# The fold's masked matrix made one pair earlier, PSUM evacuations more steps behind, and two expert downs moved to the end

## The chip, the cores and the metric

The kernel runs on one core of a Trainium2 chip. The metric is the device time of one execution in microseconds (us), the median of several runs. Profiles are of a single execution on that core.

## What is computed

A batch of 256 tokens with 1024 features goes through a first block (a mixer, attention to a memory, a layer of experts) and then two layers of a second block. The change concerns the experts of the first block alone:

```python
def hier_moe(h, w_rg, b_rg, w_re, b_re, w_gate, w_up, w_down):
    # every token picks 1 of 4 groups, in it 2 of 8 experts, with weights
    ...
    def expert_block(args):
        xb, e = args
        return (jax.nn.silu(xb @ w_gate[e]) * (xb @ w_up[e])) @ w_down[e]
    ...
    out = jnp.zeros((T, D), jnp.float32).at[t_sorted].add(contrib)   # weighted sum per token
```

There are 32 experts; w_gate and w_up are 1024x512 each, w_down 512x1024, all fp32. The second block's filters (sines of a small network, then a Fourier transform of 256 points as matrix products) depend on no token, and the kernel computes their spectra beside the experts.

## The kernel before

**Pairs.** Experts e and e+16 form a pair j (0 to 15). The 128 rows of a TensorE operand hold 64 slots of token features twice, rounded part and remainder, so that one pass over a weight gives both. `features` gathers tokens into the slots of four experts by a matmul with a 0/1 matrix `Dm` that `chosen` makes; its result is copied by ScalarE from PSUM to `XT`. `up` multiplies a pair's slots by gate (i = 0) and up (i = 1) weights, eight steps each; `gate` adds the two parts of the product and takes Silu into `G`, and `gated` multiplies `G` by the up product. `fold` is a matmul of `G` by a small matrix `F`: it transposes `G` and puts each slot to the expert it belongs to, since a crowded expert may use its partner's slots. `F` (128x128) is the table `fold` masked by `mine[:, j]`, two VectorE instructions. The fold's product is copied to `AT` as rounded part (ScalarE) and remainder (VectorE). `down` multiplies by the down weights in two halves of four steps; `result` copies each half to `Y`; `combine` multiplies `Y` by the weights and places of the tokens (`DT`, made by `weighted`: a VectorE mask, a transpose, a copy) into four PSUM sums that stay open over all pairs.

**Steps.** The work is emitted in 24 steps per pair j: 0 to 15 are `up(j)`, 16 to 23 `down(j-1)`. A step is: `go_on()`, which resumes delayed pieces that are due; `self.weights`, which asks for one weight half; four matmuls of 512 columns; then the pieces that `plan` holds for this step. A piece is a generator: `yield n` lets it go on n steps later. Within an engine the instructions run in the order in which they were emitted (`manual_schedule`).

**Weight halves.** A load brings 1 MB (128x2048 fp32) to one of nine places. Each half of it (128x1024) is split: ScalarE rounds it into `whi` (line 454, five buffers) and VectorE subtracts into `wlo` (line 455, four buffers). At step s the halves up to that of step s+4 have been asked for (`NH` = 5), so a piece started in the plan of step s stands on ScalarE and VectorE behind the half for step s+4, and one that `go_on` resumes at step s behind the half for step s+3. A place is loaded anew when both of its halves are split; the order of loads is the list `self.stream`, which follows `DOWN`.

**PSUM.** Four tiles `acc` hold the sums; two tiles `tp` serve features, transposes, folds and filters in turn; two tiles `misc` serve the products of `up` and `down` in turn.

**Slots of the plan.** `WHEN` gives the steps: features 6, 9, 12, 15 in even pairs and 14, 16, 18, 20 in odd ones; transposed weights from 1, 4, 7, 10 in pairs 1, 3, 7, 11; filter pieces at 8 and 14 of pairs 1 to 10; combines of pair j-2 at 3, 5, 7, 9; `fold(j-1)` at 0 and, for the last pair, at 16. A filter piece may issue loads on SyncE's queue (`decay`, lines 1280 and 1281) and stores on ScalarE's (lines 1315 and 1316, after a memset on VectorE, line 1314).

Lines to follow: 454 and 455 the split, 875 features' copy, 886 the masks for transposes, 899 to 909 gate and gated, 915 and 916 F, 921 the fold's matmuls, 927 and 929 its copies, 934 results, 940 combines, 960/961 and 977/978 the matmuls of up and down.

Of the kernel before, what the change touches and what calls it, by code (L numbers as in the profile page):

```python
# [22 lines left out]
F32 = mybir.dt.float32  # L23
# [4 lines left out]
OP = mybir.AluOpType  # L28
# [3 lines left out]
P = 128  # L32
# [3 lines left out]
SLOTS = 64  # L36
# [31 lines left out]
def _cols(v):  # L68
# [12 lines left out]
PAIRS = NE // 2  # L81
MEMBERS = [m * PAIRS + j for j in range(PAIRS) for m in range(2)]


WHEN = dict(features=((0, 6), (0, 9), (0, 12), (0, 15), (1, 14), (1, 16), (1, 18), (1, 20)), chosen=2,
            weighted=(1, 4, 7, 10), filters=(8, 14), combine=(3, 5, 7, 9))

DOWN = lambda j: (j - 1,) if j else ()


def _constants():
# [158 lines left out]
class Kernel:  # L250
# [246 lines left out]
    def block1(self, outer, moe):  # L497
# [3 lines left out]
        with ExitStack() as ctx:  # L501
# [218 lines left out]
            for j in range(PAIRS + 1):  # L720
                if j < PAIRS:
                    self.stream.extend(("w_egu", 8 * j + 4 * m + 2 * i + n)
                                       for i in range(2) for m in range(2) for n in range(2))
                for d in DOWN(j):
                    self.stream.extend(("w_ed", 4 * d + 2 * m + n) for n in range(2) for m in range(2))
# [86 lines left out]
    def moe(self, hh, hl, A, W):  # L812

        nc, tc = self.nc, self.tc
        mm = nc.tensor.matmul
        x = self.x
        with ExitStack() as ctx:
# [3 lines left out]
            a = ctx.enter_context(tc.tile_pool(name="moe", bufs=1, reuse_waits="tile"))  # L821
            rk = a.tile([P, 2, NE], F32, name="rk")
            mine = a.tile([P, PAIRS], F32, name="mine")
# [27 lines left out]
                    else:  # L851
                        start(work)

            XT, DT, Dms, G, AT, Y = {}, {}, {}, {}, {}, {}

            def chosen(q):

# [7 lines left out]
            def features(q, k):  # L865

                if k % 2 == 0:
                    XT[q].append(a.tile([P, 2, 4, 2, SLOTS], F32R, name="XT", bufs=6))
                ps = self.tp()
                for i, h in enumerate((hh, hl)):  # L870
                    for t in range(2):
                        mm(ps[:, i * S:(i + 1) * S], h[:, t, k * P:(k + 1) * P],
                           Dms[q][:, t].rearrange("p e j -> p (e j)"), start=t == 0, stop=t == 1)
                yield 1
                nc.scalar.activation(XT[q][k // 2][:, k % 2].rearrange("p e i j -> p i e j"),  # L875
                                     ps.rearrange("p (i e j) -> p i e j", i=2, j=SLOTS), AF.Copy)

            def weighted(o, t, h):


                if t == h == 0:
                    DT[o] = self.junk.tile([P, 4, S], F32, name="DT", tag="xn", bufs=2)
                Dw = a.tile([P, 2, 2, SLOTS], F32, name="Dw")
                for n in range(2):
                    j = 4 * o + 2 * h + n
                    nc.vector.tensor_scalar(Dw[:, n], self.c["slot"][:, None, :].to_broadcast([P, 2, SLOTS]),
                                            rp[:, t, j:j + 1], wp[:, t, j:j + 1], op0=OP.is_equal, op1=OP.mult)
                yield 2
                ps = self.tp()
                for n in range(2):  # L890
                    nc.tensor.transpose(ps[:, n * P:(n + 1) * P], Dw[:, n].rearrange("p i j -> p (i j)"), self.ident)
                yield 1
                nc.scalar.activation(DT[o][:, 2 * h:2 * h + 2, t * P:(t + 1) * P],
                                     ps[:, :2 * P].rearrange("p (n s) -> p n s", s=P), AF.Copy)

            def gate(j, p):
                yield 1
                z = a.tile([SLOTS, 512], F32, name="z")
                nc.scalar.activation(z, p[SLOTS:], AF.Copy)
                yield 1  # L900
                nc.vector.tensor_add(z, p[:SLOTS], z)
                yield 2
                G[j] = a.tile([P, 512], F32, name="g")
                for n in range(2):
                    nc.scalar.activation(G[j][n * SLOTS:(n + 1) * SLOTS], z, AF.Silu)

            def gated(j, p):
                yield 1
                nc.vector.tensor_mul(G[j], G[j], p)

            def fold(j):


                F = a.tile([P, 2, SLOTS], F32, name="F")
                nc.vector.tensor_scalar(F[:, 0], self.c["fold"], mine[:, j:j + 1], None, op0=OP.mult)
                nc.vector.tensor_sub(F[:, 1], self.c["fold"], F[:, 0])  # L916
                yield 2
                g = G.pop(j)
                pt = self.tp()
                for f in range(4):  # L920
                    mm(pt[:, f * P:(f + 1) * P], g[:, f * P:(f + 1) * P], F.rearrange("p m j -> p (m j)"),  # L921
                       start=True, stop=True)
                yield 1
                AT[j] = a.tile([P, 4, 2, 2, SLOTS], F32R, name="at", bufs=2)
                at = AT[j].rearrange("p f m i j -> p (f m) i j")
                pt = pt.rearrange("p (f j) -> p f j", j=SLOTS)
                nc.scalar.activation(at[:, :, 0], pt, AF.Copy)
                yield 1
                nc.vector.tensor_sub(at[:, :, 1], pt, at[:, :, 0].bitcast(F32))

            def result(j, n, p):
                yield 1
                Y[j, n] = a.tile([P, 512], F32, name="ye", bufs=2)
                nc.scalar.activation(Y[j, n], p, AF.Copy)

# [2 lines left out]
            def combine(j, t, n):  # L938

                mm(sums[t][n], DT[j // 4][:, j % 4, t * P:(t + 1) * P], Y[j, n], start=j == 0, stop=j == PAIRS - 1)  # L940
                yield 1

            def twice(work):
                n = 1
                while n:
                    n = next(work)
                    yield n
# [18 lines left out]
            def down(j, plan):  # L966
                at = AT.pop(j)
                for n in range(2):
                    p = self.misc()
                    for s in range(4):  # L970
                        m, h = divmod(s, 2)
                        go_on()
                        wh, wl = self.weights("w_ed", 8 * j + 4 * m + 2 * n + h)
                        for k in range(2):
                            l = at[:, 2 * h + k, m].rearrange("p i j -> p (i j)")
                            c = slice(k * 512, k * 512 + 512)
                            mm(p, l, wh[:, c], start=s == k == 0, stop=False)  # L977
                            mm(p, l, wl[:, c], start=False, stop=s == 3 and k == 1)  # L978
                        for work in plan[16 + 4 * n + s]:
                            start(work)  # L980
                    start(result(j, n, p))
# [14 lines left out]
            for j in range(PAIRS + 1):  # L996
                q, r = divmod(j, 2)
                plan = [[] for n in range(24)]
                if j == 0:
                    for k in range(2, 8):  # L1000
                        plan[k // 2 - 1].append(features(0, k))
                elif j < PAIRS:
                    plan[0].append(fold(j - 1))
                if j == PAIRS - 1:
                    plan[16].append(fold(j))
                if j == 1 or j % 4 == 3 and j < PAIRS - 1:
                    for n, s in enumerate(WHEN["weighted"]):
                        plan[s].append(weighted((j + 1) // 4, n // 2, n % 2))
                if q < last:
                    if r == 0:  # L1010
                        plan[WHEN["chosen"]].append(chosen(q + 1))
                    for k, (rr, s) in enumerate(WHEN["features"]):
                        if rr == r:
                            plan[s].append(features(q + 1, k))
                if 1 < j < PAIRS:
                    for n in range(2):
                        for t in range(2):
                            plan[WHEN["combine"][2 * n + t]].append(combine(j - 2, t, n))
                for s in WHEN["filters"]:
                    if 0 < j < PAIRS and len(todo) > KEEP:  # L1020
                        if len(todo) == 12:
                            next(spectra[1])
                        plan[s].append(todo.popleft())
                if j < PAIRS:
                    up(j, plan)
                else:
                    for n in range(2):
                        plan[17 + n].extend(combine(j - 2, t, n) for t in range(2))
                    plan[23].extend(combine(j - 1, t, 0) for t in range(2))
                for d in DOWN(j):  # L1030
                    down(d, plan)


            g, g2 = self.gains
# [199 lines left out]
    def features(self, room):  # L1234


        nc = self.nc
        F = 64
        H = self.hidden
# [457 lines left out]
```

## Time and profile before

| what | us |
|---|---|
| median of 3 runs | 1762.99 (1761.9 to 1764.7) |
| the profiled execution | 1761.24 |
| its span, first to last instruction | 1759.4 |
| TensorE matmul busy | 1653.8 (94%) |
| VectorE busy | 1293.6 (74%) |
| ScalarE busy | 1138.4 (65%) |
| first matmul of the first fold | 292.02 |
| first matmul of the last fold | 832.56 |

The expert stage with its 16 pairs is roughly a third of the span. The shares above are means over the whole span, so the stage has to be read by itself: how long one pair takes (from one fold to the next), who is idle in it and what ends that idleness. A busy TensorE is not one at its peak, since matmul rows overlap; the start of one row to the start of the next tells more. The granted clock (PEclk) is a share of 2.4 GHz and has two levels here, 0.5 and 1.

### The profile page before, as it was taken

The page shows a single profiled execution, that of the slowest core. Times are in us where ns is not written, and L with a number is a line of the kernel's source. Part 1 is how long each engine was busy: PE and PEld are TensorE (multiplying, and loading weights), DVE is VectorE, ACT ScalarE, POOL GpSimd, SP SyncE. Part 2 cuts the span into 40 slices and gives each one's busy share as a digit, 9 for nine tenths or more (in the row PEclk, how much of TensorE's full clock was granted, in tenths as well). Part 3 has the DMA queues.
Part 4 walks back from the last instruction along what each step waited for, and adds up shares of the span by engine and source line. Part 5 has one row for each costly group of instructions (what it writes and reads, how often), then busy time and mean ns, then how long its engine had stood idle before and what let it go on. Part 6 is the DMA issues. An engine that isn't in the chain of part 4 may idle for free. (4 is left out here: it accounts for less than half of the span.)

```text
span 1759.4 us, 24723 instructions
## 1 busy us (share of the span) xinstructions
PE 1653.8 (94%) x9115; PEld 1391.7 (79%) x9115; DVE 1293.6 (74%) x1702; ACT 1138.4 (65%) x1576; POOL 30.3 (2%) x47
## 2 busy tenths in 40 slices
PE   7999978999899999898899999999999999999998
PEld 6898866767667666666689987899878998789986
DVE  7976568788878789898757866677655787667763
ACT  7865448778777778887657655555545675556552
POOL 1000000000000000000000000000000000000000
PEclk9999989999999999999999999999999999999999
DMA  8645537898998889999376455455656645645551
GB/s 286 207 160 198 186 144 298 321 343 328 365 342 320 339 321 374 378 367 385 116 243 223 141 188 203 167 183 181 205 166 228 230 155 180 202 156 182 181 191 72
DMA packets 94447, 415.91 MB, mean 236 GB/s; under 512 B 12324, under 2 KB 18868, under 8 KB 68468
## 3 DMA queue, kind: packets, MB, share of 16 engines
q1 hardware_dynamic: 89220, 405.91, 64.8%
q0 software_dynamic: 864, 6.29, 1.0%
q10 hardware_dynamic: 4240, 2.10, 0.4%
q8 instruction: 73, 1.20, 0.3%
q14 instruction: 50, 0.41, 0.1%
HBM read 411.12 MB, written 3.15 MB: 235 GB/s over the span
## 5 line engine op out<-in xcount | busy, mean ns | idle before, releaser
L455 DVE TENSOR_TENSOR wlo<-raw,whi 128x1024 fp32r<-128x1024 f32 x709 | 848.6, 1221 | 268.4 <-PE acc L332 83.0
L454 ACT ACTIVATE whi<-raw 128x1024 fp32r<-128x1024 f32 x711 | 728.5, 1055 | 230.2 <-PE acc L333 118.4
L337 PE MATMUL acc<-hh,wlo 128*128 128x256 f32 x1024 | 290.1, 283 | 0.0
L336 PE MATMUL acc<-hl,whi 128*128 128x256 f32 x1024 | 290.1, 283 | 0.0
L335 PE MATMUL acc<-hh,whi 128*128 128x256 f32 x1024 | 289.9, 283 | 0.0
L960 PE MATMUL misc<-whi,XT 128*128 128x512 f32 x512 | 237.8, 464 | 2.4 <-ACT XT L875 1.4
L961 PE MATMUL misc<-wlo,XT 128*128 128x512 f32 x512 | 213.9, 418 | 1.1 <-DVE wlo L455 1.1
L335 PEld LDWEIGHTS acc<-hh,whi 128*128 128x128 f32 x1024 | 196.7, 192 | 0.1
L336 PEld LDWEIGHTS acc<-hl,whi 128*128 128x128 f32 x1024 | 196.7, 192 | 0.0
L337 PEld LDWEIGHTS acc<-hh,wlo 128*128 128x128 f32 x1024 | 196.7, 192 | 0.0
L961 PEld LDWEIGHTS misc<-wlo,XT 128*128 128x128 f32 x512 | 102.0, 199 | 41.0 <-DVE wlo L455 11.9
L960 PEld LDWEIGHTS misc<-whi,XT 128*128 128x128 f32 x512 | 102.4, 200 | 35.6 <-issue 13.2
L331 PE MATMUL acc<-whi,hh 128*128 128x512 f32 x288 | 113.6, 396 | 0.5 <-ACT hh L422 0.5
L332 PE MATMUL acc<-wlo,hh 128*128 128x512 f32 x288 | 113.5, 395 | 0.1
L333 PE MATMUL acc<-whi,hl 128*128 128x512 f32 x288 | 112.8, 392 | 0.0
L978 PE MATMUL misc<-wlo,at 128*128 128x512 f32 x256 | 104.9, 410 | 3.9 <-DVE wlo L455 3.9
L977 PE MATMUL misc<-whi,at 128*128 128x512 f32 x256 | 103.2, 403 | 0.0
L921 PE MATMUL tp<-F,g 128*128 128x128 f32 x128 | 25.1, 358 | 47.3 <-DVE F L916 47.3
L978 PEld LDWEIGHTS misc<-wlo,at 128*128 128x128 f32 x256 | 48.7, 190 | 24.5 <-DVE wlo L455 14.9
L940 PE MATMUL acc<-ye,DT 128*128 128x512 f32 x128 | 66.6, 607 | 0.0
L331 PEld LDWEIGHTS acc<-whi,hh 128*128 128x128 f32 x288 | 54.6, 190 | 12.9 <-ACT hh L422 1.2
L921 PEld LDWEIGHTS tp<-F,g 128*128 128x128 f32 x128 | 21.5, 254 | 53.9 <-issue 47.1
(466 smaller groups left out, 2791.1 us busy)
## 6 DMA issues: line engine op xcount, KB each, us to landing
raw<-in_w_egu SPq DMA_DIRECT2D x128, 1024.0 KB, 5.4
raw<-in_w_ed SPq DMA_DIRECT2D x64, 1024.0 KB, 6.7
raw<-in_w_up SPq DMA_DIRECT2D x80, 512.0 KB, 4.3
raw<-in_w_gate SPq DMA_DIRECT2D x48, 512.0 KB, 4.5
raw<-in_w_down SPq DMA_DIRECT2D x44, 512.0 KB, 4.5
raw<-in_w_qk SPq DMA_DIRECT2D x24, 512.0 KB, 6.5
raw<-in_w_out SPq DMA_DIRECT2D x24, 512.0 KB, 3.7
raw<-in_w_br SPq DMA_DIRECT2D x24, 512.0 KB, 4.1
```

The costliest lines, as they stand in the source:

```text
L331: mm(out, xh, wh, start=start, stop=False)
L332: mm(out, xh, wl, start=False, stop=False)
L333: mm(out, xl, wh, start=False, stop=stop)
L335: mm(out, wh, xh, start=start, stop=False)
L336: mm(out, wh, xl, start=False, stop=False)
L337: mm(out, wl, xh, start=False, stop=stop)
L454: self.nc.scalar.activation(hi, src, AF.Copy)
L455: self.nc.vector.tensor_sub(lo, src, hi.bitcast(F32))
L960: mm(p, l, wh[:, c], start=s == k == 0, stop=False)
L961: mm(p, l, wl[:, c], start=False, stop=s == 7 and k == 1)
L977: mm(p, l, wh[:, c], start=s == k == 0, stop=False)
L978: mm(p, l, wl[:, c], start=False, stop=s == 3 and k == 1)
```

## The change

`F` is made by a piece of its own, `mask(j)`, at step 8 of pair j, and kept in `Fs`; `fold(j-1)` starts at step 1 of the next pair and issues its matmuls there, with no delay behind `F`. Its copy follows three steps later in place of one. Other delays between the matmuls and the copy of their PSUM tile: features 2 (those of the first four experts stay at 1), transposed weights 2 and 4 between their mask and the transpose (1 and 2 before), the gate product 3, the up product 2, results 2 (1 each before). The slots in `WHEN` move: features by about one step, transposed weights one earlier, `chosen` from 2 to 0, filter pieces to 4 and 18 in even pairs and 8 and 23 in odd ones. At the end, `down(13)` no longer runs in pair 14: pair 15 runs `up(15)`, `down(13)`, `down(14)`, and then comes `down(15)`, each later down with a plan of its own for the combines. The last fold moves from step 16 to step 22 of pair 15.

```diff
--- before.py
+++ after.py
@@ -82,10 +82,11 @@
 MEMBERS = [m * PAIRS + j for j in range(PAIRS) for m in range(2)]
 
 
-WHEN = dict(features=((0, 6), (0, 9), (0, 12), (0, 15), (1, 14), (1, 16), (1, 18), (1, 20)), chosen=2,
-            weighted=(1, 4, 7, 10), filters=(8, 14), combine=(3, 5, 7, 9))
-
-DOWN = lambda j: (j - 1,) if j else ()
+WHEN = dict(features=((0, 7), (0, 10), (0, 12), (0, 15), (1, 15), (1, 17), (1, 19), (1, 21)), chosen=0,
+            weighted=(0, 3, 6, 9), filters=((4, 18), (8, 23)), combine=(3, 5, 7, 9), mask=8, fold=1)
+
+
+DOWN = lambda j: {0: (), PAIRS - 2: (), PAIRS - 1: (PAIRS - 3, PAIRS - 2)}.get(j, (j - 1,))
 
 
 def _constants():
@@ -851,7 +852,7 @@
                     else:
                         start(work)
 
-            XT, DT, Dms, G, AT, Y = {}, {}, {}, {}, {}, {}
+            XT, DT, Dms, Fs, G, AT, Y = {}, {}, {}, {}, {}, {}, {}
 
             def chosen(q):
 
@@ -871,7 +872,7 @@
                     for t in range(2):
                         mm(ps[:, i * S:(i + 1) * S], h[:, t, k * P:(k + 1) * P],
                            Dms[q][:, t].rearrange("p e j -> p (e j)"), start=t == 0, stop=t == 1)
-                yield 1
+                yield 1 if q == 0 else 2
                 nc.scalar.activation(XT[q][k // 2][:, k % 2].rearrange("p e i j -> p i e j"),
                                      ps.rearrange("p (i e j) -> p i e j", i=2, j=SLOTS), AF.Copy)
 
@@ -885,16 +886,16 @@
                     j = 4 * o + 2 * h + n
                     nc.vector.tensor_scalar(Dw[:, n], self.c["slot"][:, None, :].to_broadcast([P, 2, SLOTS]),
                                             rp[:, t, j:j + 1], wp[:, t, j:j + 1], op0=OP.is_equal, op1=OP.mult)
-                yield 2
+                yield 4
                 ps = self.tp()
                 for n in range(2):
                     nc.tensor.transpose(ps[:, n * P:(n + 1) * P], Dw[:, n].rearrange("p i j -> p (i j)"), self.ident)
-                yield 1
+                yield 2
                 nc.scalar.activation(DT[o][:, 2 * h:2 * h + 2, t * P:(t + 1) * P],
                                      ps[:, :2 * P].rearrange("p (n s) -> p n s", s=P), AF.Copy)
 
             def gate(j, p):
-                yield 1
+                yield 3
                 z = a.tile([SLOTS, 512], F32, name="z")
                 nc.scalar.activation(z, p[SLOTS:], AF.Copy)
                 yield 1
@@ -905,22 +906,25 @@
                     nc.scalar.activation(G[j][n * SLOTS:(n + 1) * SLOTS], z, AF.Silu)
 
             def gated(j, p):
-                yield 1
+                yield 2
                 nc.vector.tensor_mul(G[j], G[j], p)
 
-            def fold(j):
-
-
-                F = a.tile([P, 2, SLOTS], F32, name="F")
+            def mask(j):
+
+                Fs[j] = F = a.tile([P, 2, SLOTS], F32, name="F")
                 nc.vector.tensor_scalar(F[:, 0], self.c["fold"], mine[:, j:j + 1], None, op0=OP.mult)
                 nc.vector.tensor_sub(F[:, 1], self.c["fold"], F[:, 0])
-                yield 2
-                g = G.pop(j)
+                yield 1
+
+            def fold(j, steps):
+
+
+                g, F = G.pop(j), Fs.pop(j)
                 pt = self.tp()
                 for f in range(4):
                     mm(pt[:, f * P:(f + 1) * P], g[:, f * P:(f + 1) * P], F.rearrange("p m j -> p (m j)"),
                        start=True, stop=True)
-                yield 1
+                yield steps
                 AT[j] = a.tile([P, 4, 2, 2, SLOTS], F32R, name="at", bufs=2)
                 at = AT[j].rearrange("p f m i j -> p (f m) i j")
                 pt = pt.rearrange("p (f j) -> p f j", j=SLOTS)
@@ -929,7 +933,7 @@
                 nc.vector.tensor_sub(at[:, :, 1], pt, at[:, :, 0].bitcast(F32))
 
             def result(j, n, p):
-                yield 1
+                yield 2
                 Y[j, n] = a.tile([P, 512], F32, name="ye", bufs=2)
                 nc.scalar.activation(Y[j, n], p, AF.Copy)
 
@@ -939,6 +943,10 @@
 
                 mm(sums[t][n], DT[j // 4][:, j % 4, t * P:(t + 1) * P], Y[j, n], start=j == 0, stop=j == PAIRS - 1)
                 yield 1
+
+            def combined(j, plan, steps):
+                for n, s in enumerate(steps):
+                    plan[s].append(combine(j, n % 2, n // 2))
 
             def twice(work):
                 n = 1
@@ -1000,9 +1008,11 @@
                     for k in range(2, 8):
                         plan[k // 2 - 1].append(features(0, k))
                 elif j < PAIRS:
-                    plan[0].append(fold(j - 1))
+                    plan[WHEN["fold"]].append(fold(j - 1, 3))
+                if j < PAIRS:
+                    plan[WHEN["mask"]].append(mask(j))
                 if j == PAIRS - 1:
-                    plan[16].append(fold(j))
+                    plan[22].append(fold(j, 3))
                 if j == 1 or j % 4 == 3 and j < PAIRS - 1:
                     for n, s in enumerate(WHEN["weighted"]):
                         plan[s].append(weighted((j + 1) // 4, n // 2, n % 2))
@@ -1012,22 +1022,21 @@
                     for k, (rr, s) in enumerate(WHEN["features"]):
                         if rr == r:
                             plan[s].append(features(q + 1, k))
-                if 1 < j < PAIRS:
-                    for n in range(2):
-                        for t in range(2):
-                            plan[WHEN["combine"][2 * n + t]].append(combine(j - 2, t, n))
-                for s in WHEN["filters"]:
+                if 1 < j < PAIRS - 1:
+                    combined(j - 2, plan, WHEN["combine"])
+                for s in WHEN["filters"][r]:
                     if 0 < j < PAIRS and len(todo) > KEEP:
                         if len(todo) == 12:
                             next(spectra[1])
                         plan[s].append(todo.popleft())
                 if j < PAIRS:
                     up(j, plan)
-                else:
-                    for n in range(2):
-                        plan[17 + n].extend(combine(j - 2, t, n) for t in range(2))
-                    plan[23].extend(combine(j - 1, t, 0) for t in range(2))
                 for d in DOWN(j):
+                    if d > PAIRS - 3:
+                        plan = [[] for n in range(24)]
+                        combined(d - 1, plan, (17, 18, 20, 21))
+                        if d == PAIRS - 1:
+                            plan[23].extend(combine(d, t, 0) for t in range(2))
                     down(d, plan)
 
 
```

## Rows read from the trace of the kernel before

**Rows 1.** Waits from 288 to 858 us: who waited for whom, total us, times, longest
```profile
PE tp L921 <- DVE F L916: 47.3, 16, 3.6
ACT at L927 <- PE tp L921: 37.0, 16, 3.8
...
ACT XT L875 <- PE tp L872: 14.7, 12, 2.2
```

**Rows 2.** Timeline around the fold at 520 us: start, us, engine, line, count, idle before
```profile
509.35 10.30 DVE L455 TENSOR_TENSOR wlo<-raw,whi 128x1024 fp32r<-128x1024 f32 x9
...
516.64 0.40 PE L960 MATMUL misc<-whi,XT 128*128 128x512 f32 x1
...
516.87 0.39 PE L961 MATMUL misc<-wlo,XT 128*128 128x512 f32 x1
519.57 0.25 DVE L915 TENSOR_SCALAR F<-cst,mine 128x64 f32<-128x64 f32 x1
519.85 0.23 DVE L916 TENSOR_TENSOR F<-cst,F 128x64 f32<-128x64 f32 x1
520.22 2.05 PE L921 MATMUL tp<-F,g 128*128 128x128 f32 x8 [2.96 <-DVE F L916]
522.31 0.60 ACT L927 ACTIVATE at<-tp 128x512 fp32r<-128x512 f32 x1 [2.87 <-PE tp L921]
522.50 0.63 PE L961 MATMUL misc<-wlo,XT 128*128 128x512 f32 x1
...
524.07 1.23 DVE L455 TENSOR_TENSOR wlo<-raw,whi 128x1024 fp32r<-128x1024 f32 x1 [2.35 <-issue]
```

**Rows 3.** Windows: length, busy us (count) of PE, PEld, DVE, ACT, POOL; PEclk, DMA share, GB/s
```profile
292.02:674.85 382.83, 345.92 (x1513) 260.69 (x1513) 316.16 (x333) 296.80 (x372) 0.00 (x0) 0.94 0.90 335
674.85:808.43 133.58, 120.48 (x504) 88.72 (x505) 122.30 (x126) 114.67 (x136) 0.00 (x0) 0.97 0.97 374
808.43:858.00 49.57, 46.51 (x180) 33.59 (x180) 39.48 (x40) 33.52 (x41) 0.00 (x0) 0.93 0.54 211
446.18:481.63 35.45, 32.49 (x148) 24.45 (x149) 30.61 (x32) 29.00 (x35) 0.00 (x0) 1.00 0.94 360
776.79:808.43 31.64, 28.23 (x112) 19.81 (x113) 29.68 (x30) 26.95 (x30) 0.00 (x0) 1.00 0.98 393
508.00:517.00 9.00, 7.71 (x28) 4.53 (x27) 9.00 (x9) 9.00 (x12) 0.00 (x0) 1.00 0.91 338
519.40:526.20 6.80, 5.98 (x19) 5.13 (x20) 3.52 (x7) 2.45 (x5) 0.00 (x0) 0.50 1.00 372
```

**Rows 4.** SyncE's queue, 288 to 858 us, waits; and the page's DMA issues (KB, landing)
```profile
SPq L295 <- DVE wlo L455: 438.3, 168, 5.8
...
SPq L1280 <- PE misc L978: 0.9, 2, 0.4
...
raw<-in_w_egu SPq DMA_DIRECT2D x128, 1024.0 KB, 5.4
```

**Rows 5.** VectorE's groups from 292.02 to 674.85: busy us, mean ns, idle before
```profile
L455 DVE TENSOR_TENSOR wlo<-raw,whi 128x1024 fp32r<-128x1024 f32 x241 | 284.6, 1221 | 66.0 <-ACT whi L454 30.6 <-issue 19.2 <-PE misc L961 9.0
L886 DVE TENSOR_SCALAR Dw<-cst,rp,wp 128x128 f32<-128x128 f32 x24 | 7.2, 341 | 0.0
L929 DVE TENSOR_TENSOR at<-tp,at 128x512 fp32r<-128x512 f32 x10 | 6.8, 684 | 0.0
```

**Rows 6.** Timeline at the end of one filter group, ScalarE and VectorE, 505 to 508 us
```profile
505.23 0.17 DVE L1314 MEMSET fk<- 1x128 f32 x1
505.43 0.52 ACTq L1315 DMA_DIRECT2D spectrum<-fk  x1
...
506.52 1.06 ACT L454 ACTIVATE whi<-raw 128x1024 fp32r<-128x1024 f32 x1 [2.42 <-issue]
507.61 1.23 DVE L455 TENSOR_TENSOR wlo<-raw,whi 128x1024 fp32r<-128x1024 f32 x1 [2.21 <-ACT whi L454]
```

## The prediction

> **What bounds the kernel now.** I read four views, in this order. First the list of waits over the expert stage (288 to 858 us): its longest item by far is TensorE waiting for one small VectorE tile, the fold matrix F, 16 times, 47.3 us, so 2.96 us each; in a second item of similar size ScalarE waits for the same fold, 37.0 us [rows 1]. Then the timeline around one fold, which shows why. VectorE is making weight halves one behind the other, nine in 10.30 us (1.144 us each); TensorE has run dry at 516.87+0.39 us. F was put into VectorE's queue at step 0 of a pair, behind the halves for the four steps ahead, and is made at 519.57 and 519.85; only then does the fold start, after 2.96 us of idleness. ScalarE, whose next instruction is the fold's evacuation, has meanwhile waited 2.87 us, and VectorE then starves for 2.35 us because ScalarE stood still [rows 2]. So one wait goes round three engines: nobody gains from the others' pause, except that VectorE gets its lead back.
>
> Third, the windows: after the pause the granted clock is 0.50, that is 1.2 GHz, from 519.4 to 526.2, and a 512-column matmul's row lengthens from 0.39 to 0.63 us [rows 2, 3]. Over the ten pairs that also compute filters (j = 1 to 10, 292.02 to 674.85) the mean clock is 0.94, over the next four 0.97 [rows 3].
>
> Fourth, who has room. A pair of the first ten takes 38.28 us; VectorE is busy 31.6 and ScalarE 29.7 of it. In the four pairs without filters a pair takes 33.4 and VectorE is busy 30.6, 92% [rows 3]. Weight loads aren't late: the loads wait for VectorE to free a buffer (438 us in 168 waits), no item of the list has a half waiting for its load, and a 1 MB load lands 5.4 us after its issue [rows 4]. So before is held by the fold's wait and its echo, with TensorE and VectorE close behind it and nearly level.
>
> **The change part by part.** Call a pair's steps 0 to 23 (16 up, 8 down). A delayed piece runs at the start of a step and so stands on its engine behind the weight halves for three steps ahead; a piece put in a plan behind those for four.
>
> *F a pair earlier.* F goes to step 8 of its own pair; the fold's matmuls go straight in at step 1 of the next, 17 steps later. The operations stay (0.25 + 0.23 us on VectorE), nothing is added. What is late next for the fold? The product G, VectorE's multiply now at step 17 behind the half for step 20, against a fold at step 25: TensorE needs half 24 by then anyhow. F has one buffer; it is overwritten at step 8 after the fold read it at step 1. So I cost the fold's wait at nothing; the cover is eight steps, and if it were gone the price would be the old 2.96 us.
>
> *Evacuations later.* The fold's copy stands 3 steps behind, features and transposed weights 2, the up products 3 and 2, the results 2. ScalarE's waits for TensorE at the fold (37.0 us) and at the features (14.7 us) [rows 1] then find the matmuls done. The cost is on buffers: two `tp` and two `misc` tiles in PSUM. `misc` is safe: the first up product is read by step 11 and its bank wanted at 16; the second at 17 and wanted at 20; the results at 21 and 25, wanted at 24 and 32. Each stands just ahead of a half that TensorE needs anyway. `tp` is tight in one place: the fold's tile is freed by VectorE's subtraction at step 5, behind the half for step 8, and wanted by the feature at step 7 (even pairs) or a transpose at 7 (pairs 1, 3, 7, 11). From nothing if VectorE leads, to a half plus the subtraction, 1.14 + 0.68 = 1.8 us [rows 2, 5]. I take 0.3 per pair: by step 7 TensorE has also done the fold and two or three combines, and VectorE regains its lead there.
>
> *Moved steps.* The early slot tables shift; the masks for transposes (24 in the ten pairs, 7.2 us) [rows 5] get four steps of cover in place of two. Filter pieces go from steps 8 and 14 to 4 and 18, or 8 and 23, so part of TensorE's extra work lands in the down steps, where VectorE is the slower engine. A piece takes its loads on SyncE's queue and its stores on ScalarE's with it. The first cost weight loads almost nothing (0.9 us in two waits) [rows 4]. The second blocks ScalarE until VectorE has reached a memset, 2.42 us with the stores' own issue, and VectorE then lacks input for 2.21 us [rows 6]. The change leaves that, six times in the ten pairs: 13 us.
>
> *Order at the end.* The downs of pairs 13, 14 and 15 run behind all ups, and the weight loads in the same order. The work is the same; the last fold gets a whole down of cover.
>
> The sum, against the profiled 1761.24 us (span 1759.4; the median of three is 1.75 above it):
> - Ten filter pairs, 382.83 us. TensorE's side: minus 10 x 2.96 of waits and minus 6% of slow clock (23) leaves 330. VectorE's side: busy 316.2 plus 13 of blocks is 329 [rows 3, 6]. Two engines this level with four halves between them don't reach either bound; pair 5, which kept the full clock, gives 35.45 - 2.96 = 32.5 [rows 3], the loaded ones more. I take 34.1 a pair, 341: **-42** (bounds -25, if half the slow clock stays and `tp` costs its mean, to -53).
> - Four pairs, 133.58 us. VectorE's busy 122.3 is the floor; with 0.8 us a pair, 125.5: **-8** (-4 to -11).
> - 808.43 to 858.00: 2.96 of wait and 7% of clock, 3.5; VectorE is idle a fifth of it anyway. **-5** (-2 to -6.5).
> - The first fold, just ahead of 292.02: **-3** (0 to -3.6).
>
> Together -58: 1761.24 - 58 = 1703, and with the 1.75 to the median **1705**. The bounds add to -31 and -74: 1732 and 1689.
>
> Two rules of the skill bear on this. In the rows the last pair before the end moved 393 GB/s, and the four pairs 374 [rows 3]; my 34.1 us a pair needs 335 x 38.28 / 34.1 = 376. The Trainium skill, "DMA: Bandwidth & Descriptors", Where 436 GB/s comes from, puts the HBM side of one core at about 358 GB/s. By that, an estimate, a filter pair couldn't be under 35.8 us and the sum would be about -30; the 374 and 393 say that the rule does not bind here. The other stands with the last rival.
>
> **The rivals.**
> *The clock keeps falling.* Half of the slow stretches stem from something other than the fold's pause. For it: pairs with features and filters show more dips than the four behind them (0.94 against 0.97). Against it: the dip shown starts at the pause itself. Price: ten pairs keep 12 to 23 us, the end 3, the TensorE side then binds: -32, 1731.
> *The wait moves to `tp`.* With VectorE just in time, 1.8 us at step 7 in eight even pairs and up to 1.14 more in the four odd ones, 26 us, and if these pauses cost clock, 10 more. -58 + 36 = -22: 1741. It decides by VectorE's lead at step 7.
> *Loads bind.* A filter pair moved 335 GB/s at a share of 0.90; at 1.00 that is 372 GB/s, 34.5 us a pair, and the four pairs shrink by 3% only: -38 - 4 - 8, 1713. It lies in my range.
> *VectorE's floor.* All slack is used and the blocks shrink by half: -75, 1688.
> *Slower: the half clock in the down steps.* In down steps TensorE works 4 x 0.233 = 0.93 us (start to start, 516.64 to 516.87) [rows 2] and waits until VectorE's 1.144 are over. From 508 to 517 it was busy 7.71 of 9.00 us, and the clock stayed 1.00 [rows 3]. Without the fold's pause VectorE never gets a lead at once, so such steps go on through the start of the next pair. If the chip answered with 1.2 GHz, a down step would take 1.87 us: 8 x (1.87 - 1.14) = 5.8 a pair, 15 pairs, 87 us; less the 58 gained, +29: 1792. It decides from about ten pairs on. The Trainium skill, "TensorE: Matmul & The Clock Gate", A second HAM failure mode: psum-queue depth-cycling, tells of just this, a clock that swings when TensorE idles briefly and often between groups in PSUM; the 1.00 of 508 to 517 speaks against it here.
> *It doesn't do what it says:* F early, but the fold waits for G: excluded by the eight steps, except with a stall of VectorE behind a filter.
>
> **How the numbers follow.** My forecast with loads binding inside it: 0.72 (1694 to 1720). The clock keeps falling 0.10. `tp` 0.07. VectorE's floor 0.05. Slower 0.04; no effect 0.02. The range takes in the bounds and the clock rival, leaving out the `tp` case, the slow one and the tail of the floor: 1689 to 1732. A measurement of this kernel tells about 0.2% (3.5 us) from no change: faster 0.93, same 0.03, slower 0.04.
>
> **What would show it.** In the changed profile the item "fold waits for F" should vanish, and ScalarE's wait for the fold with it; granted clock at least 0.98 over the pairs; fold to fold 33 to 35 us in the first ten, 31 to 32 in the next three; VectorE busy about 93 to 96%. ScalarE's 2.2 to 2.4 us before a spectrum store should remain. I am wrong if TensorE waits at step 7 for the subtraction, or if the clock still dips each pair, or if weight halves begin to wait for loads.

## The result and the profile after

The changed kernel takes 1703.88 us (median of 4 runs, 1702.07 to 1706.44), the kernel before, run beside it, 1762.45 us. The ratio is 0.9672 with a 95% interval of 0.9648 to 0.9695. The forecast was 1705 us, between 1689 and 1732. The profiled execution of the changed kernel took 1706.44 us, the slowest of its four, with a span of 1704.6.

Line numbers move: the split is now 455 and 456, the gate's multiply 910, F 915 and 916, the fold's matmuls 925, its copies 931 and 933, the up matmuls 968 and 969, the down matmuls 985 and 986. The first view is the windows of the changed kernel, columns as in [rows 3]: the ten filter pairs from the first to the eleventh fold, the three pairs after them, pair 14 (which has no down now), and pair 15.

```profile
293.39:628.37 334.98, 326.98 (x1513) 251.06 (x1513) 309.06 (x328) 291.11 (x369) 0.00 (x0) 0.99 0.95 378
628.37:720.66 92.29, 90.16 (x393) 66.41 (x392) 91.46 (x97) 85.82 (x106) 0.00 (x0) 1.00 1.01 413
720.66:744.08 23.42, 20.17 (x82) 14.00 (x80) 23.21 (x25) 21.41 (x25) 0.00 (x0) 0.99 1.01 420
744.08:770.51 26.43, 24.48 (x93) 17.15 (x93) 23.68 (x24) 21.47 (x25) 0.00 (x0) 0.94 0.97 382
```

The ten pairs take 334.98 us where [rows 3] show 382.83, at a granted clock of 0.99 in place of 0.94. In the three pairs behind them VectorE is busy 91.46 of 92.29 us: it has become the limit there, and loads come at 413 GB/s.

The waits of the changed kernel from 285 to 800 us, to be read against [rows 1]:

```profile
ACT whi L455 <- PE misc L968: 23.2, 27, 3.9
PEld misc L969 <- DVE wlo L456: 21.7, 47, 1.1
DVE wlo L456 <- ACT whi L455: 20.2, 33, 2.5
...
PE tp L925 <- DVE g L910: 7.0, 2, 3.9
```

TensorE's wait for F (47.3 us) is gone, and so are ScalarE's for the fold (37.0) and the features (14.7). What stands in their place is a scatter of short waits of TensorE for single weight halves (47 times, at most 1.1 us), as one expects behind a busy VectorE. But one line is new: two folds wait for the product G, 7.0 us together. The timeline shows the first of them; the other is at 744.08 (3.03 us).

```profile
292.56 0.68 DVE L910 TENSOR_TENSOR g<-g,misc 128x512 f32<-128x512 f32 x1
293.39 2.04 PE L925 MATMUL tp<-F,g 128*128 128x128 f32 x8 [3.94 <-DVE g L910]
296.75 1.06 ACT L455 ACTIVATE whi<-raw 128x1024 fp32r<-128x1024 f32 x1 [3.88 <-PE misc L968]
297.04 1.23 DVE L456 TENSOR_TENSOR wlo<-raw,whi 128x1024 fp32r<-128x1024 f32 x1 [2.67 <-issue]
```

It is the old picture of [rows 2] with G in F's role: TensorE waits, then ScalarE and VectorE wait for TensorE. By the trace's records VectorE's queue stands from 292.04 until a matmul of line 969, which frees a `wlo` buffer, ends at 296.96. The reason is in the order of work. Pairs 0 and 14 have no down between their up and the next pair, so the multiply, delayed by two steps, comes at step 1 of the next pair, where the fold comes too.

SyncE's queue has a second new line, against [rows 4]. In the kernel before, from 285 to 858 us:

```profile
SPq L295 <- DVE wlo L455: 444.3, 170, 5.8
...
SPq L295 <- DMA spectrum<-fk: 3.9, 2, 2.3
```

In the changed kernel, from 285 to 800 us:

```profile
SPq L296 <- DVE wlo L456: 352.3, 160, 5.2
SPq L296 <- DMA spectrum<-fk: 36.1, 5, 10.9
```

Weight loads now wait up to 10.9 us for a filter's store to land. More on that below.

To see where the whole gain lies, take the first transposes behind the experts (`tp<-cst,xn`) as a landmark: they start at 865.31 us before and at 808.43 after, 56.9 sooner. What follows them takes 894.1 us before and 896.2 after; the other kernels below have 894 to 898. Nothing in the change touches that part, and the four spans of the changed kernel differ by 4.3 us, so I leave these 2 us unexplained.

### The profile page after: what moved, and what is told of

It is laid out like the page before. It is cut to its first block, busy times and chain, and to the rows that moved or that the text cites. A ratio compares the mean times of both kernels' runs of the same rounds, so it can differ in the third digit from the quotient of the medians.

```text
span 1704.6 us, 24749 instructions
## 1 busy us (share of the span) xinstructions
PE 1635.3 (96%) x9115; PEld 1380.2 (81%) x9115; DVE 1288.6 (76%) x1702; ACT 1133.9 (67%) x1576; POOL 30.3 (2%) x47
## 5 line engine op out<-in xcount | busy, mean ns | idle before, releaser
L968 PE MATMUL misc<-whi,XT 128*128 128x512 f32 x512 | 227.5, 444 | 1.1 <-ACT XT L876 1.1
L969 PE MATMUL misc<-wlo,XT 128*128 128x512 f32 x512 | 208.5, 407 | 5.2 <-DVE wlo L456 5.1
L969 PEld LDWEIGHTS misc<-wlo,XT 128*128 128x128 f32 x512 | 97.9, 191 | 47.7 <-DVE wlo L456 22.4
L968 PEld LDWEIGHTS misc<-whi,XT 128*128 128x128 f32 x512 | 98.1, 192 | 30.4 <-issue 8.9
L334 PEld LDWEIGHTS acc<-whi,hl 128*128 128x128 f32 x288 | 54.2, 188 | 11.6 <-DVE hl L424 0.7
L333 PEld LDWEIGHTS acc<-wlo,hh 128*128 128x128 f32 x288 | 54.4, 189 | 11.3 <-DVE wlo L456 0.5
```

What stands on the lines that cost most here:

```text
L333: mm(out, xh, wl, start=False, stop=False)
L334: mm(out, xl, wh, start=False, stop=stop)
L969: mm(p, l, wl[:, c], start=False, stop=s == 7 and k == 1)
```

## Experiments: which part carries the gain

**The mask alone.** The kernel before with F made at step 8 of its own pair, all else as it was:

```diff
+            def mask(j):
+                Fs[j] = F = a.tile([P, 2, SLOTS], F32, name="F")
+                ...
             def fold(j):
-                F = a.tile([P, 2, SLOTS], F32, name="F")
-                ...
                 yield 2
-                g = G.pop(j)
+                g, F = G.pop(j), Fs.pop(j)
...
+                if j < PAIRS:
+                    plan[8].append(mask(j))
```

> The kernel before with one part of the change: F is made at step 8 of its own pair; the fold's matmuls stay at step 2 of the next pair and every copy stays one step behind. Theory (the wait for F and the half clock behind it carry the gain of 59 us): the 16 waits of 2.96 us go, granted clock over the ten filter pairs rises from 0.94 to 0.98 or more, 1705 to 1715 us. Rival (the later copies carry half of it, since ScalarE otherwise waits for the fold and for the features as before): 1730 to 1740 us, with ScalarE's wait for the fold's matmuls still near 20 us or more in total.

Measured: 1714.49 us, ratio 0.9733 (0.9717 to 0.9749). Of the 59 us this part alone gives 47, near the upper end of the times that the theory expected. Its window over the ten pairs:

```profile
290.39:633.32 342.93, 328.62 (x1513) 247.13 (x1513) 311.13 (x331) 292.87 (x372) 0.00 (x0) 1.00 0.95 371
```

The ten pairs take 342.93 us with the clock at 1.00. The stores stand here where they stood before, yet SyncE waits longer for them (285 to 790 us), 25.5 us in place of 3.9:

```profile
SPq L295 <- DMA spectrum<-fk: 25.5, 3, 9.2
```

**All but the mask.** The changed kernel with F made in the fold again:

```diff
             def fold(j, steps):
-                g, F = G.pop(j), Fs.pop(j)
+                F = a.tile([P, 2, SLOTS], F32, name="F")
+                nc.vector.tensor_scalar(F[:, 0], self.c["fold"], mine[:, j:j + 1], None, op0=OP.mult)
+                nc.vector.tensor_sub(F[:, 1], self.c["fold"], F[:, 0])
+                yield 2
+                g = G.pop(j)
```

> The changed kernel with one part undone: F is made in the fold itself again (put at step 1, matmuls two steps behind), the later copies, the slots and the order at the end stay. Theory (F's wait carries the gain): TensorE waits about 3 us for F in all 16 folds, the clock dips behind them, 1745 to 1760 us. Rival (the later copies carry half): 1725 to 1740 us.

Measured: 1769.86 us, ratio 1.0058 (1.0041 to 1.0075): slower than before, beyond what either theory expected. Its waits from 285 to 860 us:

```profile
ACT whi L455 <- PE misc L972: 85.9, 49, 5.6
PE tp L929 <- DVE F L924: 56.2, 16, 5.8
```

F is waited for as before, 56.2 us in 16 folds instead of 47.3. On top of the mask the rest of the change gives -10.6 us (1714.49 to 1703.88), without it +8.8. The two profiled executions differ by 7.3 us, and not in the ten pairs: these take 379.87 us, 3.0 less than before. From the fourteenth fold to the landmark it is 4.3 us more (88.52 to 92.79), and behind the landmark, where nothing was changed, 3.8 more (894.1 to 897.9). So while F is late the rest gives little in the pairs, and part of the 8.8 is not its doing.

**The copies back.** The changed kernel with every copy out of PSUM one step behind its matmuls again:

```diff
-                yield 1 if q == 0 else 2
+                yield 1
...
-                yield 4
+                yield 2
...
-                    plan[WHEN["fold"]].append(fold(j - 1, 3))
+                    plan[WHEN["fold"]].append(fold(j - 1, 1))
```

(and in the same way for the transposed weights, the gate and up products and the results).

> The changed kernel with every copy out of PSUM one step behind its matmuls again (and the transposes two behind their mask); F stays early, slots and order at the end stay. Theory: ScalarE again waits for features and folds, but it has room (it is busy under 90% of a pair), so little is lost: 1704 to 1714 us. Rival (the later copies are needed): 1725 us or more.

Measured: 1714.8 us, ratio 0.9745 (0.9728 to 0.9763), just above what the theory expected: the later copies are worth 11 us, all that the mask alone leaves. Which of them carry it was not tried apart. The ten pairs stand at the mask's figure:

```profile
290.46:633.16 342.70, 329.48 (x1513) 250.54 (x1513) 311.44 (x331) 292.84 (x371) 0.00 (x0) 0.99 0.95 372
```

So the moved slots, the fold one step sooner and the order at the end, which this kernel keeps, add nothing that shows here.

**TensorE kept busy in the wait.** The kernel before with eleven matmuls that do no work put ahead of each fold, so that the wait for F stays and the clock doesn't fall:

```diff
                 pt = self.tp()
+                for n in range(11):
+                    mm(pt, hh[:, 0, :P], hh[:, 0, :512], start=True, stop=True)
                 for f in range(4):
```

> The kernel before with eleven matmuls of 512 columns that do no work put ahead of each fold's matmuls (2.6 us at the full clock), into the fold's own PSUM tile: TensorE is busy while it would wait for F. It takes the clock's fall away and leaves the wait. Theory (about 20 of the 48 us in the ten pairs were the clock): granted clock 0.99, the waits for F shrink to under 1 us but the fold starts no sooner, 1735 to 1745 us. Rival (the slow clock costs nothing, since VectorE has to catch up anyway): 1758 to 1768 us.

Measured: 1742.54 us, ratio 0.9897 (0.9881 to 0.9914): more work on TensorE, and 18.5 us faster. The window of the ten pairs:

```profile
292.98:656.39 363.41, 352.57 (x1623) 266.14 (x1622) 314.97 (x333) 295.79 (x372) 0.00 (x0) 1.00 0.93 351
```

382.83 us become 363.41, and the clock goes from 0.94 to 1.00. In 12 of the 16 folds TensorE still waits for F behind the added matmuls, 0.4 us at most, so there they delay no fold; in the other four no wait shows. This prices the two halves of the wait apart: 19.4 us of the ten pairs were the half clock behind the pause, a further 20.5 (363.41 to 342.93) the pause itself, 8 the later copies.

**The downs in turn.** The changed kernel with the order at the end undone:

```diff
-DOWN = lambda j: {0: (), PAIRS - 2: (), PAIRS - 1: (PAIRS - 3, PAIRS - 2)}.get(j, (j - 1,))
+DOWN = lambda j: (j - 1,) if j else ()
...
-                    plan[22].append(fold(j, 3))
+                    plan[18].append(fold(j, 1))
```

> The changed kernel with the order at the end undone: down(13) in pair 14 and down(14) in pair 15 again, one down at the end, the last fold at step 18. Theory (the order at the end moves work and changes no sum; it gives the last fold cover but takes it from the fold of pair 14, which waits 3.03 us in the changed kernel): within 4 us of the changed kernel, 1700 to 1708 us. Rival (the two downs at the end are needed): 1710 us or more.

Measured: 1701.41 us, ratio 0.9664 (0.9644 to 0.9684), against 0.9672 for the changed kernel: no difference that can be told. The order at the end brings nothing; from the fourteenth fold to the landmark this run takes 83.99 us, the changed kernel 87.77.

## Experiments: what binds now

**More for VectorE.** The changed kernel with F made four times over:

```diff
+                for n in range(4):
                     nc.vector.tensor_scalar(F[:, 0], ...)
                     nc.vector.tensor_sub(F[:, 1], ...)
```

> The changed kernel with F made four times over at step 8, six small VectorE instructions more in each of 16 pairs, about 6 x 0.24 = 1.4 us a pair, 23 us. Theory (VectorE binds): 1720 to 1728 us. Rival (TensorE or the loads bind): under 1711 us.

Measured: 1728.79 us, ratio 0.9818 (0.9803 to 0.9833), 25 us more for some 23 us of work. The ten pairs:

```profile
293.04:641.11 348.07, 333.46 (x1513) 250.00 (x1514) 323.21 (x388) 291.76 (x369) 0.00 (x0) 0.98 0.94 364
```

VectorE's busy time grows by 14.2 us, the stretch by 13.1.

**More for TensorE.** The changed kernel with five matmuls that do no work ahead of each fold:

```diff
                 pt = self.tp()
+                for n in range(5):
+                    mm(pt, hh[:, 0, :P], hh[:, 0, :512], start=True, stop=True)
```

> The changed kernel with five matmuls of 512 columns that do no work ahead of each fold's own, 5 x 0.233 = 1.17 us a pair on TensorE, 18.7 us over 16. Theory (VectorE binds, and TensorE has slack in a pair): 1704 to 1711 us. Rival (TensorE binds): 1718 to 1724 us.

Measured: 1707.07 us, ratio 0.9689 (0.9671 to 0.9708), 3 us more for 18.7 us of work. Two of the sixteen groups fall into the waits for G and hold the clock up there (the first fold starts at 291.47, 1.9 us sooner). The thirteen pairs behind the first fold take 3.2 us more (337.21 and 93.30 us in place of 334.98 and 92.29) for some 15 us of work. So VectorE binds, and TensorE has slack.

**The two folds later.** The changed kernel with the folds that wait for G at step 6:

```diff
-                    plan[WHEN["fold"]].append(fold(j - 1, 3))
+                    plan[WHEN["fold"] + 5 * (j in (1, PAIRS - 1))].append(fold(j - 1, 3))
```

> The changed kernel with the folds of pairs 0 and 14, which have no down between their up and their fold, at step 6 of the next pair in place of 1. In the changed profile these two folds wait 3.94 and 3.03 us for the product G, and the clock dips behind both. Theory (a wait of TensorE with its dip costs about 2.96 + 1.7 us where TensorE binds): both waits go, 1695 to 1700 us against 1704. Rival (VectorE binds there, so only its idle time behind the folds, 2.67 and 2.54 us, is worth something): 1699 to 1703 us.

Measured: 1697.72 us, ratio 0.9644 (0.9628 to 0.9660). Both waits are gone; 6 us is the theory's figure, at the edge of what the intervals can tell. In the profiled execution the first fold and pair 1 give 3.5 us together, and the stretch behind the fourteenth fold 2.7.

**The stores later.** In the kernel before, ScalarE stands still at the end of a filter group until VectorE has reached the memset [rows 6]. The changed kernel with the stores three steps behind the memset:

```diff
             nc.vector.memset(k[0:1, 2], 0.0)
+            if self.apart:
+                yield 3
             nc.scalar.dma_start(self.spectrum[l][:, :, gs], k)
```

> The changed kernel with the two stores at the end of a filter group three steps behind the memset they wait for, while the pairs run. Theory (VectorE binds; it loses 2.2 us at each of seven such ends because ScalarE stands still): 7 x 2.2 = 15 us at most, 1690 to 1697 us. Rival (TensorE or the loads bind in the filter pairs, so that VectorE's idle time there is free): 1701 to 1706 us.

Measured: 1701.1 us, ratio 0.9662 (0.9649 to 0.9675): the rival's number. Yet its windows (pairs 1 to 6, pair 7, pairs 8 to 10) say that the theory was right in the main and part of the gain was lost again in one place:

```profile
291.29:484.57 193.28, 192.37 (x904) 150.66 (x905) 184.10 (x197) 174.38 (x222) 0.00 (x0) 0.98 0.95 380
484.57:527.34 42.77, 36.67 (x162) 28.10 (x160) 33.52 (x40) 29.54 (x40) 0.00 (x0) 0.88 0.93 367
527.34:622.40 95.06, 94.93 (x449) 74.41 (x448) 91.15 (x93) 87.73 (x109) 0.00 (x0) 1.00 0.95 382
```

Pairs 1 to 6 and 8 to 10, which hold all six stores, take 288.3 us, against 299.2 in the changed kernel (334.98 less 35.80 for its pair 7); but pair 7 takes 42.77. There TensorE waits 6.1 us for a filter's weight (the waits of that stretch, then SyncE's timeline):

```profile
PE tp L1305 <- DMA w<-in_filt_w: 6.1, 1, 6.1
```

```profile
481.48 12.46 SPq L296 DMA_DIRECT2D raw<-in_w_ed  x3
494.03 0.38 SPq L1285 DMA_DIRECT2D w<-in_filt_w  x1
```

SyncE took 12.46 us to issue three weight loads, and the small load stood behind them. Why the three? The trace's records name the semaphore (a counter on the chip) that each load or store signals when it lands. Those from SyncE and ScalarE take eight semaphores in turn, and in the 80 cases of this run where the records are complete, none was issued before the last one on its semaphore had landed. A store that lands late so holds up the weight load that shares its semaphore, and with it SyncE's queue: here a spectrum store issued at 480.40 us landed at 493.07, and the load on its semaphore was issued at 493.13, after 11 us in which SyncE issued nothing. These waits came to 36.1 us in the changed kernel and to 51.3 in this one.

**Both edits.**

> The two edits together, the later folds and the later stores. If each is worth what its own run shows, their sum: theory 1684 to 1692 us, rival 1698 to 1703 us.

Measured: 1694.21 us, ratio 0.9622 (0.9609 to 0.9635): the sum of what the two runs gained (6.2 and 2.8 us), and 2 us above the theory's range; pair 7 takes 43.05 us here as well.

**The stores from GpSimd.** The later folds, and the stores issued by GpSimd, which is idle in this stage and whose DMAs signal on semaphores of their own in the trace:

```diff
-            nc.scalar.dma_start(self.spectrum[l][:, :, gs], k)
-            nc.scalar.dma_start(self.nyquist[l][:, gs], k4)
+            nc.gpsimd.dma_start(self.spectrum[l][:, :, gs], k)
+            nc.gpsimd.dma_start(self.nyquist[l][:, gs], k4)
```

> The changed kernel with the two folds at step 6 and the stores at the end of a filter group issued by GpSimd, which is idle there, in place of ScalarE. Theory (the stores cost twice: ScalarE stands still for the memset, and a later weight load waits for a store to land because they share one of eight completion semaphores, 36 us of SyncE's waits in the changed kernel and 57 in the run with both edits): pair 7 loses its 10 us stall of that run, 1682 to 1689 us. Rival (the loads' late start is covered by the nine places, and pair 7's stall is another matter): 1692 to 1698 us.

Measured: 1684.26 us, ratio 0.9562 (0.9543 to 0.9581), the fastest of all, 20 us below the changed kernel. SyncE no longer waits for a spectrum, and pair 7 takes 33.38 us in place of 43.05, which is nearly all that this kernel gains on the run with both edits. Its windows: pair 2, pairs 4 to 6, and pairs 11 to 13:

```profile
321.49:353.11 31.62, 31.62 (x150) 24.74 (x149) 30.27 (x32) 29.97 (x37) 1.43 (x2) 1.00 1.01 410
...
385.46:481.08 95.62, 95.60 (x450) 74.17 (x448) 91.56 (x94) 88.03 (x111) 3.25 (x5) 1.00 1.00 407
...
609.52:701.82 92.30, 90.18 (x394) 66.38 (x392) 91.47 (x97) 85.83 (x106) 0.00 (x0) 1.00 1.00 404
```

In the filter pairs TensorE's rows now fill the window (31.62 of 31.62) with VectorE at 96%; in the pairs without filters VectorE is at 99%. The two engines have met. The DMA engines are busy all the time too (1.00 and 1.01); whether they would bind next was not tried.

**The masks on GpSimd too.** F and the masks for the transposes made by GpSimd:

```diff
-                nc.vector.tensor_scalar(F[:, 0], self.c["fold"], mine[:, j:j + 1], None, op0=OP.mult)
-                nc.vector.tensor_sub(F[:, 1], self.c["fold"], F[:, 0])
+                nc.gpsimd.tensor_scalar(F[:, 0], self.c["fold"], mine[:, j:j + 1], None, op0=OP.mult)
+                nc.gpsimd.tensor_tensor(F[:, 1], self.c["fold"], F[:, 0], op=OP.subtract)
...
-                    nc.vector.tensor_scalar(Dw[:, n], self.c["slot"]...
+                    nc.gpsimd.tensor_scalar(Dw[:, n], self.c["slot"]...
```

> The kernel with later folds and GpSimd's stores, and now F and the masks for transposes made by GpSimd too, taking 16 x 0.47 and 32 x 0.30 us, 17 us in all, off VectorE. Theory (VectorE alone binds the pairs): up to 17 us less than that kernel, 1670 to 1677 us. Rival (TensorE is close behind, or GpSimd's work slows VectorE's): 1680 us or more.

Measured: 1704.09 us, ratio 0.9681 (0.9667 to 0.9695): 20 us slower than the run before it. Its windows of pairs 2 and 3, and GpSimd's groups:

```profile
321.17:352.79 31.62, 31.62 (x150) 24.74 (x149) 30.02 (x30) 29.85 (x37) 4.03 (x4) 1.00 0.99 383
352.79:395.44 42.65, 36.42 (x157) 27.80 (x156) 31.66 (x31) 30.74 (x42) 19.42 (x11) 0.88 0.84 324
```

```profile
L915 POOL TENSOR_SCALAR F<-cst,mine 128x64 f32<-128x64 f32 x15 | 59.6, 3975 | 208.6 <-PE tp L925 208.6
L887 POOL TENSOR_SCALAR Dw<-cst,rp,wp 128x128 f32<-128x128 f32 x30 | 51.0, 1706 | 46.9 <-PE tp L892 46.9
```

And TensorE's wait for the masks, 285 to 800 us:

```profile
PE tp L892 <- POOL Dw L887: 17.6, 9, 3.3
```

Pair 2, which makes no transposes, takes 31.62 us with or without F on VectorE: TensorE is the limit there. Pair 3 takes 42.65 for 32.35, because a mask now takes 1.7 us in place of 0.34, and TensorE waits for it; the clock falls behind that (0.88). The rival's number came true, and so did its first half, that TensorE is close behind. Its second did not: VectorE's subtraction of a half takes 1221 ns here and 1216 in the run before. What cost the time, the masks' 1.7 us on GpSimd, neither the theory nor the rival named.

## Why the prediction was right, and where it was not

**The main term.** The ten pairs gave 47.9 us (382.83 to 334.98) where 42 were forecast, between 25 and 53. The mask alone gives 39.9 of them, the later copies the rest. The two parts of the wait are confirmed apart: the clock, put at 23 by the windows, measured 19.4 with TensorE kept busy; the pause, 29.6 of TensorE's idleness, measured 20.5. That VectorE used the rest of the pause to regain its lead is likely and not shown. The step from the two bounds to a time above both held: 334.98 lies between 330 and the 341 that was taken.

One reading was wrong, and the sum does not use it: "VectorE then starves for 2.35 us because ScalarE stood still". By the trace's records VectorE's queue stood from 520.04 until a matmul of line 961, which frees a `wlo` buffer, ended at 523.99. VectorE, too, waited for TensorE.

**The later copies** were given no term of their own: they were to let ScalarE's waits find the matmuls done, at a cost of 0.3 us a pair on `tp`. They are worth 11 us. No wait at step 7 for the subtraction shows in the changed profile, so the 0.3 was nothing, and the rival that moves the wait to `tp` didn't come.

**The first fold: wrong.** Forecast -3, measured +1.4 (292.02 to 293.39). The step that failed reads "What is late next for the fold? The product G ... at step 17 ... against a fold at step 25", and the rival on G "excluded by the eight steps". The eight steps are a down's, and pairs 0 and 14 have none before the next pair: the diff's own DOWN says so. The old price, 2.96 us, came back at both places (3.94 and 3.03), and putting those two folds at step 6 recovers 6 us. It is the later copies, the multiply among them, that cost it: with the mask alone the first fold starts at 290.39, with the copies back at 290.46, 3 us sooner than in the changed kernel.

**The four pairs and the end.** Forecast -8 and -5. From the eleventh fold to the fourteenth, three pairs, the time went from 101.94 (674.85 to 776.79) to 92.29 us: -9.7, more than the -8 put down for four, since VectorE came closer to its floor (99% busy) than assumed. From the fourteenth fold to the landmark only 0.8 came (88.52 to 87.77): the wait for G at 744.08 and its dip (0.94) sit in there. "The last fold gets a whole down of cover" is true, but the fold of pair 14 lost its own. The terms, -47.9 - 9.7 - 0.8 + 1.4, make -57 where -58 was forecast. That the sum comes so near is luck: the ten pairs gave 5.9 us more than forecast, the first fold and the end 6.9 less.

**Moved steps: half wrong.** "A piece takes its loads on SyncE's queue and its stores on ScalarE's with it" was the right question. That ScalarE's block would stay was right: VectorE still stands 2.2 to 2.5 us at each of the six stores. The store's effect on the weight loads was not seen at all: 3.9 us before, 36.1 after, and in the runs with later stores it cost 10 us in pair 7. Nor is it the moved steps that bring it. With the mask alone, the stores unmoved, it is 25.5 us; with all but the mask, the stores moved, 7.9 (285 to 860 us). It grows where the pairs get shorter, and the stores then land later: 3.5 to 7.0 us after their issue in the kernel before, 4.8 to 7.6 with the mask alone, 5.8 to 9.5 in the changed one. Issuing the stores from GpSimd removes both, the block and the wait.

**The rivals.** Loads do not bind in the ten pairs: they come at 378 GB/s there, at 413 and 420 behind them, above the 393 of [rows 3]. In the three pairs at 413 the DMA share is 1.01, so they have no room left; but with F made four times over these pairs take 97.25 us in place of 92.29, so VectorE binds there. The Trainium skill, "DMA: Bandwidth & Descriptors", Where 436 GB/s comes from, puts the HBM side of one core at about 358 GB/s; this trace does not agree, with 413 over 92.29 us. The clock hardly kept falling. Over the ten pairs it was 0.99; away from the folds it fell in pairs 6 and 7 (0.95 in each), the first time behind a wait of 1.35 us at 489.44 for a half that a store's block had delayed. The half clock in down steps did not appear: 47 short waits for halves, and the granted clock was 1.00 from 628 to 720 us. The Trainium skill, "TensorE: Matmul & The Clock Gate", A second HAM failure mode: psum-queue depth-cycling, tells of a clock that swings when TensorE idles briefly and often; the 1.00 does not agree with that. VectorE's floor was named at 1688; with the blocks gone the fastest run stands at 1684. Of the signs that the prediction named, F's wait and ScalarE's went and the clock rose; VectorE is busy 92% of the ten pairs and 99% of the next three, where 93 to 96% was said.

## What to carry to other kernels

When one engine waits for a small operation of another, look where that operation stands in the other's queue: with a lookahead of four halves, a request made two steps ahead of its use is late by design, and making it a stage earlier cost nothing here. Price such a pause with its echo, the waits on the engines it holds up and the slow clock behind it, and check the cover for every iteration, the first and last above all. When a stage gets shorter, follow its stores as well as its loads, up to the semaphore they signal on: what landed in time before may be late now.

## What the runs showed of the hardware

Work that does nothing made the kernel before faster: eleven empty matmuls in each pause kept the granted clock at 1.00 and took 18.5 us off. DMA moved 420 GB/s over 23.42 us, nearly all of it loads of 1 MB. GpSimd took 3975 ns for a 128x64 multiply by a scalar that VectorE does in 248, and 1706 against 341 for the 128x128 mask, so an idle GpSimd was no free place for them; issuing stores from it was.
